# Attention scores in another PSUM pool, a second order for the last tiles' memory branch, and the sample recurrence's buffers swapped so that a weight load moves up

## The chip, the cores and the metric

The kernel runs on one core of a Trainium2 chip. The metric is the device time of one execution, in microseconds (us). Five engines run side by side: TensorE (PE, matmuls; PEld is its weight load), VectorE (DVE), ScalarE (ACT), GpSimd (POOL) and SyncE (SP, which here issues DMAs). Each works through its own instructions in order and waits on semaphores for the others.

## The reference, cut to what matters

One layer of a hybrid decoder for a prompt of 1,024 tokens and for 8 sequences of one new token each ("samples"). One projection of the normed input feeds three groups: NSA attention (8 query heads, 2 key/value heads; compressed blocks, selected blocks and a window of 512, mixed by gates), an RWKV-7 recurrence (4 heads) and attention into 256 memory tokens (4 heads). The groups are multiplied by SiLU gates, concatenated and projected out. The parts that the change touches:

```python
def masked_softmax(s, mask):                  # compressed, selected and window scores
    s = jnp.where(mask, s, -jnp.inf)
    m = jnp.max(s, axis=-1, keepdims=True)
    p = jnp.exp(s - m)
    return p / jnp.maximum(jnp.sum(p, axis=-1, keepdims=True), 1e-30)

def compress(rows2, pe, w1, b1, w2, b2):      # w1 is "w1a" in the kernel
    lo = einsum('ecpgd,epdh->ecgh', ch + pe[:, None, :CMP_STRIDE, None, :], w1[:, :CMP_STRIDE])
    hi = einsum('ecpgd,epdh->ecgh', ch + pe[:, None, CMP_STRIDE:, None, :], w1[:, CMP_STRIDE:])
    hid = silu(lo[:, :-1] + hi[:, 1:] + b1)
    ...
def step(s, inp):                             # RWKV-7, one token
    sa = einsum('bhvk,bhk->bhv', s, -kk_t)
    s = s * w_t + sa * b_t + v_t * k_t
    return s, einsum('bhvk,bhk->bhv', s, r_t)
# y is then normed per head, scaled, and a bonus r*k*r_k*v is added
```

## The kernel before, in words

The program has three phases. Phase 1 (to about 511 us) projects the prompt and runs its recurrence. Phase 2 (511 to 807 us) is the prompt's attention. Phase 3 (807 to the end) is the output projection, with the NSA attention of the 8 samples woven in.

**Phase 2.** The prompt has 8 tiles of 128 tokens, worked from tile i = 7 down to 0. Each tile has four units (2 key/value heads g, 2 head pairs hp), so there are 32 units n = 0 to 31. For a unit, `attn_scores` multiplies queries and keys into PSUM (p_s, in pieces of up to 512 keys; a split in high and low parts makes three matmuls of one product), VectorE masks them and takes the running maximum (`mask`, L1389, tile nm), ScalarE takes exp (L1399), VectorE the reciprocal of the sum (`scale`, L1403, tile fac), and POOL multiplies by it and by the gate (L1406). TensorE then transposes the probabilities (p_pT; `pt_copy` L1351 copies them to SBUF on ScalarE, L1360, or VectorE, L1362, as `self.turn` says) and multiplies by the values (p_o, L1447). Per tile there is also `attn_cmp` (compressed scores p_sc; VectorE's maximum L1324 and subtraction L1327 into pcq), `attn_rwkv` (p_yT) and `attn_mem` (memory scores p_sm; maximum nm_m L1484, exp into pmem L1486, POOL's scaling L1489, transposition p_pTm, copies ptm L1497, product p_om, addition to cat L1512).

PSUM has eight banks in phase 2: pool pS has two buffers of two banks for p_s, pool pT three of one bank for every transposition and, through the name pM, for p_sc, p_sm, p_om and others, and pO has one for p_o. A tile's buffer is reused only when all readers of its former tenant are done.

The order of the work is made in `phase2` (L1561). The units run in a loop; four generators are stepped between them at given rates: `query_tasks` (queries, compressed scores of the next tile), `tile_tasks` (recurrence output and memory branch of a tile), and `sample_tasks` with `sample_rest` (the samples' memory and window attention and their recurrence). Each yields the time that its step should have before the next is taken. `until(j, name)` steps generator j until it has reported `name`. The class `InOrder` keeps TensorE's instructions in the order in which they were written; the other engines are ordered by a scheduler's priorities.

**The samples.** `sample_rwkv` (L2142) is the recurrence of the 8 samples. It uses three SBUF arenas of 128 x 2048 (tags k0 to k2): a0 holds the state and a product, a1 (arena 1) the product t2, the inputs vk and the output column yv, a2 (arena 2) the rows vr and y. Its output goes through DRAM (sy_d) into another layout y, is normed (VectorE, L2280 and on) and transposed (p_sy). `nsa_ahead` (L1952), run behind it, loads what the samples' NSA attention needs first: the page table, the weights w1a into arena 2 (four DMAs, L1020), and the pages of sample 0, which a page table addresses: x (compressed rows) in arena 0 and kv in arena 1 (`pages`, L1937, L1950). SP issues these DMAs in its program order, and an issue that must wait for its target's readers holds up those behind it.

**Phase 3.** `sample_nsa` (L1966) loads the output weights as wraw (eight of 256 KB, L2299; cast and split into woh and wol at L2300 and L2301), v_new, then sample 1's pages and so on, all through SP. TensorE computes p_new, the compression of sample 0 (p_hid: pages times w1a), then output tiles of the prompt (p_out) with the compression of further samples between them.

## Time and profile before

| | us |
|---|---|
| median of 3 runs (lowest, highest) | 959.92 (959.6, 960.62) |
| profiled execution, its own time | 957.99 |
| span of that execution in the trace | 956.1 |

The mean granted clock of TensorE over the span is 0.990. The profile comes from the one execution in the third row. Busy times are per engine; a row of the timeline gives start, duration, engine, line, operation, written tile and read tiles, how many instructions it joins, and in brackets how long the engine stood idle before it and what released it. TensorE's instructions are recorded at L88 or L85 (the helper), so its rows are read by the tiles' names. The granted clock (1.00 is full) is the last but two of a table's columns; a DMA share of 1.00 means that all 16 DMA engines were busy.

### The profile page before, as it was taken

The page shows a single profiled execution, that of the slowest core. Times are in us where ns is not written, and L with a number is a line of the kernel's source. Part 1 is how long each engine was busy: PE and PEld are TensorE (multiplying, and loading weights), DVE is VectorE, ACT ScalarE, POOL GpSimd, SP SyncE. Part 2 cuts the span into 40 slices and gives each one's busy share as a digit, 9 for nine tenths or more (in the row PEclk, how much of TensorE's full clock was granted, in tenths as well). Part 3 has the DMA queues.
Part 4 walks back from the last instruction along what each step waited for, and adds up shares of the span by engine and source line. Part 5 has one row for each costly group of instructions (what it writes and reads, how often), then busy time and mean ns, then how long its engine had stood idle before and what let it go on. Part 6 is the DMA issues. An engine that isn't in the chain of part 4 may idle for free.

```text
span 956.1 us, 25353 instructions
## 1 busy us (share of the span) xinstructions
PE 907.5 (95%) x10095; PEld 754.5 (79%) x10095; DVE 650.5 (68%) x2146; ACT 431.8 (45%) x973; POOL 179.0 (19%) x262
## 2 busy tenths in 40 slices
PE   7999999999999999999997989999989988999998
PEld 7998888868898887778875767777877776787976
DVE  6668579847593799563447877677776895448564
ACT  7664324232442243222444666557567765324311
POOL 2000000000000000000001444444354765112111
PEclk9999999999999999999999999999999999999999
DMA  8521304321331127136327433240120043986561
GB/s 273 133 68 34 102 14 120 91 57 44 103 89 49 35 67 172 49 99 170 105 89 193 171 97 116 90 140 3 49 84 7 11 134 105 320 270 209 189 237 46
DMA packets 134989, 105.96 MB, mean 111 GB/s; under 512 B 34673, under 2 KB 121272, under 8 KB 134744
## 3 DMA queue, kind: packets, MB, share of 16 engines
q1 hardware_dynamic: 129880, 92.64, 32.7%
q0 software_dynamic: 3200, 10.49, 3.1%
q8 instruction: 79, 1.29, 0.6%
q10 hardware_dynamic: 1792, 1.23, 0.5%
q14 instruction: 38, 0.31, 0.1%
HBM read 85.74 MB, written 22.78 MB: 113 GB/s over the span
## 4 chain that ended last, share of the span: by engine, by line
PE 72%; DVE 16%; ACT 5%; DMA 3%; issue 3%; SPq 0%; POOL 0%; DVEq 0%; ACTq 0%; POOLq 0%
PE p_pr L88 19%; PE p_out L88 9%; PE p_pr L309 7%; PE p_o L88 5%; PE p_pT L88 5%; PE p_s L88 5%; PE p_hid L88 3%; DVE p L1389 3%; ACT p L1399 2%; PE p_iy L88 2%; PE p_z L88 1%; PE p_it L88 1%; PE p_mo L1137 1%; DVE wlo L286 1%; DMA w1a<-in_cmp_w_dram 1%
## 5 line engine op out<-in xcount | busy, mean ns | idle before, releaser
L88 PE MATMUL p_pr<-h,whi 128*128 128x512 f32 (+2 forms) x976 | 238.7, 337 | 0.0
L88 PEld LDWEIGHTS p_pr<-h,whi 128*128 128x128 f32 x976 | 157.7, 189 | 16.7 <-issue 2.8
L88 PE MATMUL p_pr<-h,wlo 128*128 128x512 f32 (+2 forms) x488 | 157.5, 326 | 0.6 <-DVE wlo L286 0.6
L1406 POOL TENSOR_SCALAR p<-p,fac,gates 128x640 f32<-128x640 f32 (+7 forms) x128 | 106.4, 843 | 126.8 <-DVE fac L1403 69.9
L1399 ACT ACTIVATE p<-p,nm 128x640 f32<-128x640 f32 (+7 forms) x128 | 92.7, 727 | 20.1 <-DVE nm L1389 18.2
L88 PEld LDWEIGHTS p_pr<-h,wlo 128*128 128x128 f32 x488 | 91.6, 189 | 9.1 <-DVE wlo L286 0.8
L88 PE MATMUL p_pT<-ident,p 128*128 128x128 f32 x528 | 72.4, 283 | 7.0 <-ACT pt L1360 2.5
L1389 DVE CUSTOM_DVE_ANT_0 p<-p_s,bmask 128x512 f32<-128x512 f32 (+3 forms) x128 | 64.4, 534 | 15.5 <-PE p_s L88 11.9
L1058 POOL MEMSET w2d<- 128x128 f32 x1 | 0.2, 205 | 393.0 <-PE p_yy L88 393.0
L88 PEld LDWEIGHTS p_pT<-ident,p 128*128 128x128 f32 x528 | 58.0, 143 | 19.0 <-issue 7.6
L309 PE MATMUL p_pr<-h,whi 128*128 128x264 f32 (+2 forms) x320 | 69.7, 311 | 0.0
L88 PE MATMUL p_o<-pt,vs 128*64 128x128 f32 x1056 | 68.8, 279 | 0.6 <-DVE cat L1464 0.6
L1360 ACT ACTIVATE pt<-p_pT 128x512 f32<-128x512 f32 (+1 forms) x82 | 46.9, 583 | 45.8 <-PE p_pT L88 45.5
L88 PEld LDWEIGHTS p_o<-pt,vs 128*64 128x64 f32 x1056 | 57.8, 138 | 9.1 <-issue 6.0
L286 DVE TENSOR_TENSOR wlo<-wraw,whi 128x1024 fp32r<-128x1024 f32 x33 | 40.4, 1223 | 31.7 <-ACT whi L285 31.7
L285 ACT ACTIVATE whi<-wraw 128x1024 fp32r<-128x1024 f32 x34 | 36.0, 1058 | 48.4 <-PE p_pr L88 35.7
L309 PEld LDWEIGHTS p_pr<-h,whi 128*128 128x128 f32 x320 | 51.4, 189 | 2.4 <-issue 0.2
L88 PE MATMUL p_out<-woh,chi 128*128 128x512 f32 x128 | 51.7, 404 | 0.0
L1362 DVE COPY pt<-p_pT 128x512 f32<-128x512 f32 (+1 forms) x62 | 41.1, 669 | 15.2 <-PE p_pT L88 15.0
L88 PE MATMUL p_out<-woh,clo 128*128 128x512 f32 x128 | 50.2, 392 | 0.4 <-DVE clo L2327 0.4
L88 PE MATMUL p_out<-wol,chi 128*128 128x512 f32 x128 | 50.1, 391 | 0.0
L309 PE MATMUL p_pr<-h,wlo 128*128 128x264 f32 (+2 forms) x160 | 49.3, 308 | 0.0
(552 smaller groups left out, 1880.0 us busy)
## 6 DMA issues: line engine op xcount, KB each, us to landing
wraw<-in_w_in_dram SPq DMA_DIRECT2D x34, 512.0 KB
pg<-in_c_pool_dram SPq DMA_DIRECT2D x32, 256.0 KB
pg<-in_c_pool_dram SPq DMA_DIRECT2D x48, 128.0 KB
x<-in_x_prompt_dram SPq DMA_DIRECT2D x8, 512.0 KB
z_d<-zt SPq DMA_DIRECT2D x16, 256.0 KB
cat<-z_d SPq DMA_DIRECT2D x8, 512.0 KB
xres<-in_x_prompt_dram POOLq DMA_DIRECT2D x16, 256.0 KB, 3.4
out_dram<-xres POOLq DMA_DIRECT2D x16, 256.0 KB, 3.4
```

Of the source, the lines that this page charges most:

```text
L88: self.last = getattr(self.engine, op)(*a, **k)
L285: nc.scalar.activation(hi[:, :, :n], raw[:, :, :n], AF.Copy)
L286: (low or nc.vector).tensor_tensor(lo[:, :, :n], raw[:, :, :n], hi[:, :, :n].bitcast(F32), op=OP.subtract)
L309: self.last_mm = self.pe.matmul(ps[:m, :b - a], w[:, k, :m], h[k][:, a:b], start=(k == 0 and i == 0), stop=(k == 7 and i == 2))
L1058: nc.gpsimd.memset(w2d[:], 0.0)
L1137: PE.matmul(po[t][:], a, w[:, j], start=(k + j == 0 and i == 0), stop=(k + j == 7 and i == 2))
L1360: self.last_copy = nc.scalar.activation(pt[:, :n], ps[:, :n], AF.Copy)
L1362: nc.vector.tensor_copy(pt[:, :n], ps[:, :n])
L1389: V.tensor_tensor_reduce(Ps[h, b][:, c0 - start:c1 - start], ps[:, h, :w], m, -1.0, nm[:, h, b, 0:1] if n else 3.0e38, op0=OP.add, op1=OP. ...
L1399: A.activation(x, x, AF.Exp, scale=-1.0, bias=nm[:, h, b, n:n + 1], accum_out=sm[:, h, b:b + 1])
L1406: nc.gpsimd.tensor_scalar(x, x, f[:, h, b:b + 1], gate[:, hd + h, 1 + b:2 + b], op0=OP.mult, op1=OP.mult)
```

## The change

- `attn_cmp` and `attn_mem` put their scores into one buffer of pool pS (half of two banks, and two banks) in place of two buffers of pool pT.
- `scale` issues its reciprocal only behind the last mask issued so far.
- `pt_copy` gives three of four copies to ScalarE in unit 0 too, where it was every second.
- In `phase2`, at unit 25, the queries of tile 0 and the memory branch of tile 1 are finished ahead of the unit's other work, with all that lies before them in their generators.
- In `sample_rwkv`, arenas 1 and 2 change places: t2, vk and yv lie in arena 2, the rows and y in arena 1. Six yields between its steps are gone.
- `nsa_ahead` is split: page table, w1a and sample 0's x pages are issued as soon as the recurrence's output is on its way through DRAM; the kv pages (arena 1) follow behind the recurrence.
- `START` gives the sample generator 0.5 in place of 0.7 before unit 0, and one yield in `attn_cmp` is 8.0 in place of 7.0. TensorE's order up to unit 25 is the same in both kernels.

```diff
@@ -37,7 +37,7 @@
 RATE = {i: (0.8, 0.8, 1, 1) if i > 3 else (1.5, 1.5, 1.8, 0) for i in range(8)}
 WAIT = (15.0, 5.0, 5.0, 0.0, 0.0, 0.0, 3.0, 0.0)
 WARM = (16, 15)
-START = (0.34, 0.0, 0.7, 0.0)
+START = (0.34, 0.0, 0.5, 0.0)
 PACE = 0.85
 EM = math.exp(-0.5)
 
@@ -1309,9 +1309,10 @@
         gate = self.gates[:, i, :].rearrange("p (h b) -> p h b", b=3)
         x = 56 - 8 * i
         half = [slice(h * 64, h * 64 + 64) for h in range(2)]
-        p2 = [self.pM.tile([128, 2, 2, 64], F32, name="p_sc", tag="m") for _ in range(2)]
+        two = self.pS.tile([128, 2, 512], F32, name="p_sc", tag="s")
+        p2 = [two[:, h, 0:256].rearrange("p (a b c) -> p a b c", a=2, b=2) for h in range(2)]
         for ps, o in zip(p2, half):
-            PE.matmul(ps[:].rearrange("p a b c -> p (a b) c"), self.cmask[o, 120:248],
+            PE.matmul(ps.rearrange("p a b c -> p (a b) c"), self.cmask[o, 120:248],
                       bc(self.cmask[o, None, x:x + 64], [64, 4, 64]), start=True, stop=False)
         for hp in range(2):
             for g in range(2):
@@ -1321,10 +1322,10 @@
         by = lambda x: x.rearrange("p (a h b) c -> p a h b c", a=2, h=2)
         st = self.small.tile([128, 8, 1], F32, name="c_m")
         for h, ps in enumerate(p2):
-            V.tensor_reduce(by(st[:])[:, :, h, :, 0], ps[:], axis=AX.X, op=OP.max)
+            V.tensor_reduce(by(st[:])[:, :, h, :, 0], ps, axis=AX.X, op=OP.max)
         V.tensor_scalar(st[:], st[:], -1.0e20, None, op0=OP.max)
         for h, ps in enumerate(p2):
-            V.tensor_tensor(by(pcq[:])[:, :, h], ps[:], bc(by(st[:])[:, :, h], [128, 2, 2, 64]), op=OP.subtract)
+            V.tensor_tensor(by(pcq[:])[:, :, h], ps, bc(by(st[:])[:, :, h], [128, 2, 2, 64]), op=OP.subtract)
         yield
         A.activation(pcq[:], pcq[:], AF.Exp)
         sm = self.small.tile([128, 8], F32, name="c_s")
@@ -1335,7 +1336,7 @@
         V.reciprocal(rc[:], rc[:])
         V.tensor_tensor(gh, gh, gate[:, :, 0].rearrange("p (g h) -> p g h", g=2), op=OP.mult)
         (G if i < 7 else V).tensor_tensor(pcq[:], pcq[:], bc(rc[:, :, None], [128, 8, 64]), op=OP.mult)
-        yield 7.0 if i < 7 else 4.0
+        yield 8.0 if i < 7 else 4.0
         self.pcT[i] = self.pt_copy(lambda j: pcq[:, 2 * j:2 * j + 2, :].rearrange("p a b -> p (a b)"), "c")
         yield
 
@@ -1356,7 +1357,7 @@
             self.te.transpose(ps[:, j, :], src(j), self.ident[:])
         pt = self.wk.tile([128, 4, 128], F32, name="pt", tag="pt" + tag, bufs=2 if tag == "c" else PTB)
         self.turn += 1
-        if self.turn % (2 if self.unit < 16 else 4):
+        if self.turn % (2 if 0 < self.unit < 16 else 4):
             self.last_copy = nc.scalar.activation(pt[:, :n], ps[:, :n], AF.Copy)
         else:
             nc.vector.tensor_copy(pt[:, :n], ps[:, :n])
@@ -1386,7 +1387,7 @@
         def mask(ps, h, b, n, c0, c1):
             w, start = c1 - c0, w0 if b else 0
             m = self.bmask[:, 1152 - w:1152] if c1 == n1 else self.bmask[:, 0:w] if b else self.bmask[:, 128:128 + w]
-            V.tensor_tensor_reduce(Ps[h, b][:, c0 - start:c1 - start], ps[:, h, :w], m, -1.0, nm[:, h, b, 0:1] if n else 3.0e38,
+            self.last_mask = V.tensor_tensor_reduce(Ps[h, b][:, c0 - start:c1 - start], ps[:, h, :w], m, -1.0, nm[:, h, b, 0:1] if n else 3.0e38,
                                    op0=OP.add, op1=OP.min, accum_out=nm[:, h, b, n:n + 1])
 
         f = self.small.tile([128, 2, 2], F32, name="fac")
@@ -1400,7 +1401,8 @@
             self.scales.append(lambda: scale(b, w))
 
         def scale(b, w):
-            V.reciprocal(f[:, :, b], sm[:, :, b])
+            with self.tc.issue_after(self.last_mask.ins):
+                V.reciprocal(f[:, :, b], sm[:, :, b])
             for h in range(2):
                 x = Ps[h, b][:, :w]
                 nc.gpsimd.tensor_scalar(x, x, f[:, h, b:b + 1], gate[:, hd + h, 1 + b:2 + b], op0=OP.mult, op1=OP.mult)
@@ -1469,7 +1471,8 @@
         qh, ql = self.qs[i]
         V, A, G, PE = nc.vector, nc.scalar, nc.gpsimd, self.te
         pms, pts = [], []
-        banks = [self.pM.tile([128, 2, 256], F32, name="p_sm", tag="m") for _ in range(2)]
+        two = self.pS.tile([128, 2, 512], F32, name="p_sm", tag="s")
+        banks = [two[:, h].rearrange("p (c k) -> p c k", c=2) for h in range(2)]
         for c in range(2):
             for n, (q, k) in enumerate(((qh, self.mkh), (qh, self.mkl), (ql, self.mkh))):
                 for h, ps in enumerate(banks):
@@ -1481,7 +1484,7 @@
             sm = self.small.tile([128, 2], F32, name="sm_m")
             pm = self.we.tile([128, 2, 256], F32, name="pmem", tag="pmem", bufs=2)
             pms.append(pm)
-            V.tensor_reduce(nm[:], ps[:], axis=AX.X, op=OP.max, negate=True)
+            V.tensor_reduce(nm[:], ps, axis=AX.X, op=OP.max, negate=True)
             for c in range(2):
                 A.activation(pm[:, c, :], ps[:, c, :], AF.Exp, bias=nm[:, c:c + 1], accum_out=sm[:, c:c + 1])
             V.reciprocal(sm[:], sm[:])
@@ -1547,8 +1550,9 @@
         while self.jobs:
             yield 1.0
         self.done.add("win")
-        yield from self.sample_rwkv()
-        yield from self.nsa_ahead()
+        ahead = self.nsa_ahead()
+        yield from self.sample_rwkv(ahead)
+        yield from ahead
 
     def sample_rest(self):
 
@@ -1656,6 +1660,9 @@
                             self.load_z(6)
                         if i > 0 and i < 7:
                             self.load_z(i - 1)
+                    if n == 25:
+                        until(0, ("q", 0))
+                        until(1, ("mem", 0))
                     pieces = sum(4 if units[m][0] >= 4 else 2 for m in ahead(n))
                     nxt = chain(*(scores(m) for m in ahead(n)))
                 later = turn(*groups[j + 1]) if j + 1 < len(groups) else None
@@ -1957,10 +1964,13 @@
         cd = self.cd = self.cs2.tile([128, 320], F32, name="c_dc")
         nc.sync.dma_start(cd[:], I["c_dc"])
         w1 = self.arena(2, "w1a")
+        x = self.arena(0, "pg")[:]
         with self.tc.high_priority(offset=2 * FIRST):
             self.load_w1([w1[:, e * 1024:e * 1024 + 1024].rearrange("p (j s h) -> p j s h", j=8, s=2) for e in range(2)])
-        self.pg = [self.arena(k, "pg")[:] for k in range(2)]
-        self.pages(0, *self.pg)
+        self.pages(0, x=x)
+        yield
+        self.pg = x, self.arena(1, "pg")[:]
+        self.pages(0, kv=self.pg[1])
         yield
 
     def sample_nsa(self):
@@ -2139,7 +2149,7 @@
             r = 0 if o is lo else 1
             V.tensor_tensor(c, c, x.rearrange("p s (c r) -> p r c s", r=2)[:, r], op=OP.mult)
 
-    def sample_rwkv(self):
+    def sample_rwkv(self, ahead):
         tc, nc, I, O = self.tc, self.nc, self.I, self.O
         V, A, G, PE = nc.vector, nc.scalar, nc.gpsimd, self.te
         b0, b1, b2 = (self.slot(j, [128, 1024], F32, f"rw_b{j}") for j in range(3))
@@ -2212,7 +2222,7 @@
         yield from wait(9.0)
         while self.unit < 16:
             yield 1.0
-        a0, a1, a2 = (self.arena(j, f"rw_a{j}") for j in range(3))
+        a0, a1, a2 = (self.arena(j, f"rw_a{j}") for j in (0, 2, 1))
         S, t = (a0[:, n:n + 1024].rearrange("p (a b) -> p a b", b=64) for n in (0, 1024))
         nc.sync.dma_start(a0[:, 0:1024], I["state_rwkv_wkv"][0].rearrange("s h (b v) k -> (s h b) (v k)", b=4))
         t2 = a1[:, 0:1024].rearrange("p (a b) -> p a b", b=64)
@@ -2241,19 +2251,15 @@
         kb = lambda j: bc(vk[:, j:j + 1, :], [128, 16, 64])
         vb = lambda x: bc(x[:, :, None], [128, 16, 64])
         V.tensor_tensor(t, S, kb(0), op=OP.mult)
-        yield 1.0
         V.tensor_tensor(S, S, kb(4), op=OP.mult)
         yield 1.0
         V.tensor_reduce(sa, t, axis=AX.X, op=OP.add)
-        yield 1.0
         V.tensor_tensor(t2, vb(vv), kb(2), op=OP.mult)
         yield 1.0
         V.tensor_tensor(S, S, t2, op=OP.add)
-        yield 1.0
         V.tensor_tensor(t, vb(sa), kb(1), op=OP.mult)
         yield 1.0
         V.tensor_tensor(S, S, t, op=OP.add)
-        yield 1.0
         V.tensor_tensor(t, S, kb(3), op=OP.mult)
         yield 1.0
         nc.sync.dma_start(O["wkv_sample"][0].rearrange("s h (b v) k -> (s h b) (v k)", b=4), a0[:, 0:1024])
@@ -2262,6 +2268,7 @@
         yd = tc.dram_tile([128, 16], F32, name="sy_d")
         nc.sync.dma_start(yd[:], yv)
         nc.sync.dma_start(y.rearrange("p h d -> p (h d)"), yd[:].rearrange("(s q) e -> s (q e)", s=NS))
+        next(ahead)
         h4 = lambda x: x.rearrange("p (h d) -> p h d", d=64)
         b4 = lambda x: bc(x[:, :, None], [NS, 4, 64])
         bn = self.small.tile([128, 4], F32, name="sbn")[:NS]
```

## The prediction, before the change was run

> **What bounds the kernel now.** I read the page first, then a table of stages, then the waits of TensorE, and last the timeline where it stands still. From the page, the busy times and the chain that ended last:
>
> ```profile
> PE 907.5 (95%) x10095; PEld 754.5 (79%) x10095; DVE 650.5 (68%) x2146; ACT 431.8 (45%) x973; POOL 179.0 (19%) x262
> PE 72%; DVE 16%; ACT 5%; DMA 3%; issue 3%; SPq 0%; POOL 0%; DVEq 0%; ACTq 0%; POOLq 0%
> ```
>
> TensorE is the bound, and the change takes no matmul from it. What can be won is its idle time and the time at half clock, so the stages matter (stretch, its length, then busy time and count per engine, granted clock, DMA share, GB/s):
>
> ```profile
> 511.00:521.00 10.00, 4.88 (x50) 3.66 (x52) 8.36 (x26) 4.29 (x11) 2.37 (x2) 1.00 0.73 206
> 521.00:525.00 4.00, 4.00 (x22) 3.40 (x20) 4.00 (x14) 2.81 (x7) 1.73 (x2) 0.57 0.97 250
> 560.00:650.00 90.00, 84.94 (x991) 66.61 (x989) 64.97 (x226) 55.13 (x131) 40.48 (x49) 1.00 0.37 113
> 650.00:750.00 100.00, 95.07 (x1067) 75.27 (x1063) 73.67 (x262) 69.32 (x176) 50.81 (x65) 1.00 0.13 36
> 750.00:782.00 32.00, 28.30 (x329) 23.00 (x325) 30.68 (x100) 23.59 (x73) 24.12 (x29) 1.00 0.22 70
> 784.40:787.80 3.40, 3.40 (x29) 2.95 (x29) 3.40 (x18) 2.89 (x10) 0.46 (x2) 0.52 0.37 90
> 795.00:807.00 12.00, 10.95 (x143) 8.58 (x144) 6.25 (x31) 8.63 (x28) 7.28 (x15) 1.00 0.20 58
> 807.00:811.00 4.00, 0.42 (x17) 0.36 (x15) 3.09 (x5) 0.77 (x1) 1.06 (x2) 0.64 1.11 306
> 811.00:815.00 4.00, 3.52 (x16) 3.22 (x16) 0.14 (x1) 0.27 (x1) 0.00 (x0) 0.50 1.10 313
> 820.00:834.00 14.00, 13.42 (x60) 10.66 (x59) 6.25 (x8) 3.40 (x5) 3.76 (x7) 1.00 0.93 309
> ```
>
> The idle time stands in four places: the start of attention (5.1 us of ten), its middle (5.1 of 90, 4.9 of 100, 3.7 of 32), its tail, and the handover to the sample stage, where TensorE does 0.42 us of work in four. After idle it runs at half clock (0.57, 0.52, 0.50). What it waits for in the whole run, and one wait of VectorE:
>
> ```profile
> PE p_hid L88 <- DMA w1a<-in_cmp_w_dram: 4.9, 2, 3.6
> PE p_s L88 <- DVE nm L1389: 4.5, 2, 3.8
> PE p_pT L88 <- ACT pt L1360: 2.5, 2, 1.6
> PE p_pT L88 <- DVE pcq L1327: 2.5, 3, 0.9
> PE p_sc L88 <- DVE pt L1362: 1.6, 1, 1.6
> PE p_sc L88 <- ACT pmem L1486: 1.3, 1, 1.3
> PE p_om L88 <- DVE cat L1512: 1.2, 1, 1.2
> PE p_pT L88 <- POOL pmem L1489: 0.8, 1, 0.8
> DVE fac L1403 <- ACT p L1399: 13.0, 20, 2.3
> ```
>
> The six rows of p_pT, p_sc and p_om I read as waits for one of three PSUM banks, which the transposes share with the compressed and memory scores (of the one put down to POOL this is an assumption: p_sm held a bank there too). The change gives these scores the window scores' two larger buffers.
>
> **Term 1, the start.** The last wait for nm, and two places like it further on:
>
> ```profile
> 520.79 0.50 PE L88 MATMUL p_s<-kh,qh 64*128 64x512 f32 x2 [3.81 <-DVE nm L1389]
> ...
> 711.50 0.48 PE L88 MATMUL p_s<-kh,qh 64*128 64x512 f32 x2
> ...
> 754.45 0.42 PE L88 MATMUL p_s<-kh,qh 64*128 64x384 f32 x1
> ```
>
> Here VectorE is the bound (8.36 of 10 us). Moving the reciprocal behind the last mask takes a wait of about 1.3 us from it, and the copies of unit 0 that go from VectorE to ScalarE take some 0.67 us each, most of them later than 525. But p_sc now occupies one of the two p_s buffers: the third p_s behind it waits for half of the subtraction L1328, so the same 3.8 us stand one p_s earlier, less what VectorE saves. I take +0.5 us (gains are positive). The lower end is 0; the upper is +2.2, if the idle is cut so far that the 4 us at clock 0.57 stay at full speed (1.7 us).
>
> **Term 2, the middle.** Gone, or mostly: 2.5 (pcq), 1.3 (pmem behind p_sc), 0.8 (POOL pmem), and about 0.9 of the 2.5 for pt and 0.6 of p_om's 1.2, together 6.1 us. ScalarE and VectorE, busy at most 74 us in 100, have room for the reads. New: the p_s behind a p_sc. It needs the buffer of the p_s ahead of p_sc, whose second mask ends here:
>
> ```profile
> 712.98 0.69 DVE L1389 CUSTOM_DVE_ANT_0 p<-p_s,bmask 128x512 f32<-128x512 f32 x1
> ...
> 755.01 0.55 DVE L1389 CUSTOM_DVE_ANT_0 p<-p_s,bmask 128x384 f32<-128x384 f32 x1
> ...
> 786.60 0.27 DVE L1389 CUSTOM_DVE_ANT_0 p<-p_s,bmask 128x128 f32<-128x128 f32 x1
> ```
>
> That is at 713.67 and 755.56, while p_s started at 711.50 and 754.45: new waits of 2.2 and 1.1 us. At the other places I put 1.0 in all. 6.1 − 4.3 = +1.8. Ends: −1, if each of the eight p_sm makes its follower wait 0.4 us more; +4, if the stream shifts so that half of the new waits are covered by the p_o matmuls that come next.
>
> **Term 3, the tail.** TensorE's order is written by hand; before, from the compressed scores of tile 0 on:
>
> ```order
> 2853 L88 MATMUL p_sc<-cmask 128x256 x2
> 2854 L88 MATMUL p_sc<-ck,q 128x64 x8
> 2855 L88 MATMUL p_s<-kh_6273,qh 128x128 x2
> 2856 L88 MATMUL p_s<-kl_6274,qh 128x128 x2
> 2857 L88 MATMUL p_s<-kh_6273,ql 128x128 x2
> 2858 L88 MATMUL p_pTm<-ident,pmem 128x128 x4
> 2859 L88 MATMUL p_s<-kh_6273,qh 128x128 x2
> ```
>
> And in the changed kernel, TensorE again, from the same p_sc to the second p_s behind it:
>
> ```order
> 2852 L88 MATMUL p_sc<-cmask 128x256 x2
> 2853 L88 MATMUL p_sc<-ck,q 128x64 x8
> 2854 L88 MATMUL p_pTm<-ident,pmem 128x128 x8
> 2855 L88 MATMUL p_yT<-ident,y_rw 128x128 x2
> 2856 L88 MATMUL p_om<-ptm,mv 64x128 x8
> 2857 L88 MATMUL p_sm<-mkh,qh 128x256 x2
> ...
> 2863 L88 MATMUL p_pT<-ident,p 128x128 x8
> 2864 L88 MATMUL p_s<-kh_6273,qh 128x128 x2
> ...
> 2867 L88 MATMUL p_s<-kh_6273,qh 128x128 x2
> ```
>
> Tile 1's p_pTm, p_yT and p_om and tile 0's p_sm now come in one block ahead of the unit's window scores. From the timeline of before, the p_sc and what comes at the stage's end:
>
> ```profile
> 782.26 0.38 PE L88 MATMUL p_sc<-cmask 64*128 64x256 f32 x1 [1.60 <-DVE pt L1362]
> ...
> 806.94 0.25 PE L88 MATMUL p_new<-s_o,qb 128*32 128x1 f32 x11
> ...
> 810.77 3.75 PE L88 MATMUL p_hid<-pg,w1a 128*128 128x128 f32 x16 [3.58 <-DMA w1a<-in_cmp_w_dram]
> 815.80 2.02 PE L88 MATMUL p_hid<-pg,w1a 128*128 128x128 f32 x16 [1.28 <-DMA w1a<-in_cmp_w_dram]
> 817.58 0.48 PE L88 MATMUL p_out<-woh,chi 128*128 128x512 f32 x1
> ...
> 833.60 3.81 PE L88 MATMUL p_hid<-pg,w1a 128*128 128x128 f32 x32 [0.58 <-issue]
> ```
>
> Won: the 1.60 us before p_sc (its bank is now a p_s buffer, long free), the half clock behind it (3.4 us at 0.52, that is 1.6), and 1.0 of the 1.05 us idle in 795 to 807, since memory's last steps no longer stand at the end: 4.2. Lost: about 0.5 us before p_om, for the copies of p_pTm, and a stall at the second p_s. That p_s needs the buffer of the p_s right ahead of it, because p_sm holds the other; so it waits for masks that VectorE's order puts behind the additions of both p_om, sums, p_sm's maximum and a copy. Three of these are passes over 512 columns:
>
> ```profile
> L1362 DVE COPY pt<-p_pT 128x512 f32<-128x512 f32 (+1 forms) x62 | 41.1, 669 | 15.2 <-PE p_pT L88 15.0
> ...
> L1484 DVE TENSOR_REDUCE nm_m<-p_sm 128x2 f32<-128x512 f32 x16 | 10.5, 680 | 0.6 <-PE p_sm L88 0.6
> ```
>
> So three by 0.68, two masks of 0.27, and ten smaller ones that I estimate at the masks' 0.27: 5.3 us from the last p_om on, while TensorE has 1.3 (p_sm), 1.1 (p_pT) and 0.5 (p_s) us to do: a stall of 2.4. 4.2 − 0.5 − 2.4 = +1.3. Ends: −2.5 (stall 4.2 and another half-clock window), +4 (no stall).
>
> The Trainium skill (TensorE: Matmul & The Clock Gate, Part 1) says that the clock falls to half after an idle window of about 3.4 us; the row shows it behind a wait of 1.60. By that rule the half clock would not hang on this wait, the 1.6 us would stay, and the term would be −0.3; the trace speaks for the row.
>
> **Term 4, the handover.** SP's queue before (each DMA once; a page's address load left out), around the weights w1a:
>
> ```order
> 235 L1950 DMA pg<-in_c_pool_dram 128x256
> 236 L1302 DMA cat_11116<-z_d 128x8x128
> 237 L2299 DMA wraw<-in_w_out_dram 128x512
> 238 L1020 DMA w1a<-in_cmp_w_dram 128x8x64 x4
> 239 L2299 DMA wraw<-in_w_out_dram 128x512 x7
> 240 L1981 DMA v_new<-out_dram 32x2x128 x4
> 241 L1942 TENSOR_LOAD pt
> 242 L1946 ISA
> 243 L1946 DMA pg<-in_c_pool_dram 128x2x256
> ```
>
> SP's queue in the changed kernel, at w1a and then from the third key/value page on:
>
> ```order
> 200 L1957 DMA pg<-in_c_pool_dram 128x256
> 201 L1020 DMA w1a<-in_cmp_w_dram 128x8x64 x4
> 202 L2270 DMA rw_a1_10321<-sy_d 8x256
> ...
> 230 L1957 DMA pg<-in_c_pool_dram 128x256
> 231 L2306 DMA wraw<-in_w_out_dram 128x512 x8
> 232 L1991 DMA v_new<-out_dram 32x2x128 x4
> ...
> 247 L1957 DMA pg<-in_c_pool_dram 128x256
> 248 L1949 TENSOR_LOAD pt
> 249 L1953 ISA
> 250 L1953 DMA pg<-in_c_pool_dram 128x2x256
> ```
>
> w1a moves some 30 us up, since its arena now holds buffers that the recurrence drops early. What waits for the norm's last read (p_sy) instead is the eight key/value pages, and all eight wraw stand behind the first three. SP's DMA issues before (start, time until the last ends, count):
>
> ```profile
> 772.51 10.30 SPq L1950 DMA_DIRECT2D pg<-in_c_pool_dram  x15
> ...
> 804.17 3.80 SPq L1020 DMA_DIRECT2D w1a<-in_cmp_w_dram  x4
> 808.03 6.01 SPq L2299 DMA_DIRECT2D wraw<-in_w_out_dram  x7
> 815.74 2.29 SPq L1981 DMA_DIRECT2D v_new<-out_dram  x4
> 818.64 11.52 SPq L1946 DMA_DIRECT2D pg<-in_c_pool_dram  x11
> ```
>
> Count from p_new at E = 806.9. Before, p_out starts at 817.58 = E + 10.7. Without the two waits, and with 32 p_hid in 3.8 us as at 833.60, it starts at E + 4.1: 6.6 us won. But the next p_hid (16.0 us behind p_out, so wanted at E + 20.1) needs sample 1's pages. Their issue starts after p_sy (about E − 3): eight wraw at 0.86 (6.9), v_new 2.3, eight pages at 0.69 to 1.05 (5.5 to 8.4), so at E + 11.7 to E + 14.6, where it was E + 11.7: not sooner. Before, those eight pages were issued by 827.0 (E + 20.1), and were used at E + 26.7, with DMA 0.93 busy; I put their landing 4 us behind the last issue, at E + 24, and the same after. So TensorE waits 3.9 us there and keeps 6.6 − 3.9 = +2.7. Ends: −2.8 (used as late as before, and issued 2.8 later), +6.6. The y load, now behind w1a's 3.8 us of issue, stays hidden: its first reader on VectorE ran at 780 or later.
>
> **Sum.** 0.5 + 1.8 + 1.3 + 2.7 = 6.3 us off the profiled execution's 957.99 (span 956.1 and 1.9 around it): 951.7. That execution is 1.9 below the median of the runs, 959.92; off the median it is **953.6**.
>
> **Rivals.** (a) Late pages take the handover back: sample 1's pages come when they did, and the wait is long enough for 32 p_hid at half clock (1.9 us lost). 3.6 − 1.9 = 1.7 won: 958.2. For it: DMA share 0.93 and an unmoved issue time. Against: w1a's 1 MB leaves the busiest stretch. (b) Slower: the window scores run on one buffer wherever p_sc or p_sm holds the other. Price: the 3.3 us of rows 711 and 754, 0.6 us at eight p_sm (4.8), against 6.1 gained: −2.0; in the tail a stall of 4.2 with a new half-clock window: −2.5; start 0, handover +1.1. Together −3.4: 963.3. It decides from the point where the new waits, 6.7 us in the forecast (4.3 and 2.4), come to 13. For it: VectorE is busy 30.68 of 32 us before the tail, so masks come late there. Against: in most of the middle it has a quarter of its time free. (c) More: no half clock at the start (+1.7), no tail stall (+2.4), pages 1.5 us sooner: 11.9 won, 948.0. (d) The half clock at 784 does not come from the wait there and stays (by the Trainium skill's rule above): 4.7 won, 955.2. (e) The arena is not free when SP comes to w1a and the load waits for p_sy as before: without term 4, 3.6 won, 956.3; against it, the recurrence's result leaves by 771.
>
> **Chances.** Forecast 0.46, (a) 0.16, (b) 0.15, (c) 0.13, (d) 0.06, (e) 0.04. A measurement here tells 0.2% (1.9 us) from nothing; so "same" is 958.0 to 961.8, which takes half of (a): 0.08. Slower is (b): 0.15; faster the rest: 0.77. The range leaves out (b) and the far part of (c): 947.5 to 960.0.
>
> **What would show it.** Right: no wait for w1a and p_out some 4 us behind p_new; a wait of 2 to 5 us on a page at the second p_hid; p_pT no longer waiting for pcq; p_s waiting for nm in two or three new places, one in the tail. Wrong: new waits of p_s over 13 us, a p_hid at half clock behind late pages, or p_out waiting for wraw, now issued behind p_sy.

## The result, and the profile after

The changed kernel is slower: 970.61 us (median of 8 runs, 966.53 to 972.65) against 961.87 (8 runs of the kernel before, 959.6 to 964.35). The ratio is 1.0087, 95% interval 1.0065 to 1.011, so about 8.4 us. The profiled executions took 969.58 and 957.99 us; the latter lies at the lower end of the runs of the kernel before (956.89 to 967.29 over the 25 runs of one comparison), so a difference of the two traces overstates the loss by some 3 us. Its mean granted clock, 0.990, is high too: the 104 later runs of the kernel before have 0.984 in the mean, the eight of the changed kernel 0.980.

The page after, busy times and the chain that ended last:

```profile
PE 917.1 (95%) x10095; PEld 761.1 (79%) x10095; DVE 649.8 (67%) x2143; ACT 433.3 (45%) x976; POOL 176.6 (18%) x262
PE 72%; DVE 14%; ACT 4%; DMA 3%; issue 3%; SPq 3%; POOL 1%; POOLq 0%; DVEq 0%; ACTq 0%
```

TensorE does the same 10,095 matmuls and is busy 9.6 us longer: the same work at a lower clock. SP's queue is new in the chain with 3%. The stages after (columns as before):

```profile
511.00:521.00 10.00, 5.65 (x54) 3.78 (x52) 8.32 (x30) 4.63 (x9) 2.38 (x2) 1.00 0.85 248
521.00:525.00 4.00, 4.00 (x38) 3.20 (x36) 3.92 (x17) 3.69 (x7) 2.17 (x2) 1.00 1.14 334
...
650.00:750.00 100.00, 93.38 (x1001) 73.56 (x1001) 71.22 (x247) 65.69 (x165) 45.94 (x58) 0.97 0.12 35
750.00:782.00 32.00, 28.82 (x313) 23.29 (x312) 26.98 (x84) 19.70 (x60) 18.52 (x25) 0.89 0.11 34
...
820.00:834.00 14.00, 12.80 (x43) 9.41 (x44) 8.34 (x15) 6.67 (x12) 2.69 (x5) 0.76 0.84 264
834.00:860.00 26.00, 22.86 (x126) 20.13 (x125) 8.20 (x18) 5.88 (x11) 2.78 (x6) 0.93 0.94 306
```

The start has gained its full clock in this trace (1.00 where it was 0.57). The middle has lost it (0.97 and 0.89 where it was 1.00), and so has the handover (0.76 and 0.93, also 1.00 before). From 807 to 815 it is the other way round: 0.64 and 0.50 before, 1.00 now. The rows of before that the prediction does not show, one of the stages and one of TensorE's waits:

```profile
834.00:860.00 26.00, 26.00 (x175) 22.19 (x174) 10.20 (x29) 6.94 (x16) 2.70 (x5) 1.00 0.88 282
...
PE p_pT L88 <- POOL p L1406: 0.9, 2, 0.7
```

What TensorE waits for after:

```profile
PE p_s L88 <- DVE nm L1390: 6.6, 5, 2.1
PE p_pT L88 <- POOL p L1408: 4.7, 8, 1.6
PE p_out L88 <- ACT woh L2307: 3.4, 1, 3.4
PE p_hid L88 <- issue: 3.1, 1, 3.1
PE p_s L88 <- DVE pcq L1328: 3.0, 1, 3.0
...
PE p_pT L88 <- ACT pt L1361: 2.2, 1, 2.2
PE p_sm L88 <- DVE nm L1390: 1.9, 1, 1.9
PE p_s L88 <- ACT pmem L1489: 1.1, 1, 1.1
PE p_sc L88 <- DVE nm L1390: 1.0, 2, 0.8
```

The waits for w1a (4.9) and for pcq in front of p_pT (2.5) are gone, as the change meant. In their place stand waits of the scores for p_s buffers, transpositions that wait for POOL (4.7 us in 8 places, where it was 0.9 in 2), p_out for woh, and the second p_hid (put down to "issue"; the chain of waits shows a page's DMA there). And VectorE's wait for ScalarE in front of the reciprocal, which was 13.0 us, is now:

```profile
DVE fac L1405 <- ACT p L1400: 3.7, 6, 1.4
```

Lengths by marks on TensorE's timeline (first p_s of attention, first queries p_q of tile 6, p_q of tile 0, p_new, second and third p_hid, end), in us:

| from, to | before | after | difference |
|---|---|---|---|
| first p_s, first p_q | 24.5 | 22.5 | -2.0 |
| first p_q, p_q of tile 0 (the middle) | 238.4 | 249.1 | +10.7 |
| p_q of tile 0, p_new (the tail) | 32.4 | 31.7 | -0.7 |
| p_new, second p_hid | 26.7 | 29.1 | +2.4 |
| second p_hid, third | 9.1 | 10.7 | +1.6 |
| third p_hid, end | 113.4 | 114.3 | +0.9 |

In the middle TensorE's idle time rose by 2.1 us (14.0 to 16.1, from the gaps of the timeline). The rest is clock: behind five of its waits stand stretches at half clock, and the trace of before has none in the middle:

```profile
553.86:557.27 3.41, 3.41 (x26) 2.97 (x28) 2.87 (x10) 1.65 (x5) 0.00 (x0) 0.50 0.68 229
622.13:625.54 3.41, 3.41 (x23) 1.52 (x24) 2.34 (x9) 0.34 (x1) 2.36 (x4) 0.50 0.02 5
714.29:717.70 3.41, 3.41 (x30) 3.08 (x27) 2.25 (x7) 2.13 (x5) 0.00 (x0) 0.50 0.01 2
727.94:731.35 3.41, 3.41 (x18) 2.12 (x19) 2.11 (x6) 2.00 (x5) 0.00 (x0) 0.50 0.12 38
758.66:765.49 6.83, 6.83 (x48) 5.29 (x46) 5.57 (x17) 2.70 (x7) 1.30 (x2) 0.50 0.01 2
```

The waits ahead of them, from TensorE's timeline:

```profile
553.84 0.58 PE L88 MATMUL p_sm<-mkh,qh 64*128 64x256 f32 x2 [1.86 <-DVE nm L1390]
...
621.95 0.45 PE L88 MATMUL p_s<-kh,qh 64*128 64x256 f32 x2 [2.96 <-DVE pcq L1328]
...
713.11 0.51 PE L88 MATMUL p_s<-kh,qh 64*128 64x512 f32 x2 [2.04 <-DVE nm L1390]
726.38 0.66 PE L88 MATMUL p_pT<-ident,p 128*128 128x128 f32 x4 [2.22 <-ACT pt L1361]
...
757.57 0.77 PE L88 MATMUL p_pT<-ident,p 128*128 128x128 f32 x5 [1.60 <-POOL p L1408]
```

Three are waits for a p_s buffer (554, 622 and 713; only the last stands where one was forecast), one is a transposition that waits for POOL, one a transposition behind a copy on ScalarE.

Part of the +10.7 is luck of the trace of before. Seven kernels of the experiments below leave the scores' buffers and the reciprocal as they were (only_copies, only_early_w1a, only_tail_order, early_w1a_late_kv, early_w1a_kv_later and its two filled forms). By the same marks their middle takes 241.5 to 243.9 us, in the median 241.9: idle 12.2 to 13.3, and 4.7 to 7.9 lost to half clock (half of the busy time in it). So the change costs the middle some 7 us, about 3 of idle time and 5 of clock, and not 10.7.

### The profile page after: what moved, and what is told of

It reads as the page before. It is cut to its first block, busy times and chain, and to the rows that moved or that the text cites. A ratio compares the mean times of both kernels' runs of the same rounds, so it can differ in the third digit from the quotient of the medians.

```text
span 967.8 us, 25326 instructions
## 1 busy us (share of the span) xinstructions
PE 917.1 (95%) x10095; PEld 761.1 (79%) x10095; DVE 649.8 (67%) x2143; ACT 433.3 (45%) x976; POOL 176.6 (18%) x262
## 3 DMA queue, kind: packets, MB, share of 16 engines
q1 hardware_dynamic: 129880, 92.64, 32.4%
## 4 chain that ended last, share of the span: by engine, by line
PE 72%; DVE 14%; ACT 4%; DMA 3%; issue 3%; SPq 3%; POOL 1%; POOLq 0%; DVEq 0%; ACTq 0%
PE p_pr L88 21%; PE p_pr L309 7%; PE p_out L88 7%; PE p_pT L88 5%; PE p_o L88 5%; PE p_s L88 5%; DVE p L1390 2%; PE p_hid L88 2%; PE p_iy L88 2%; PE p_z L88 1%; POOL p L1408 1%; PE p_it L88 1%; PE p_tk L88 1%; DVE wlo L286 1%; ACT p L1400 1%
## 5 line engine op out<-in xcount | busy, mean ns | idle before, releaser
L1408 POOL TENSOR_SCALAR p<-p,fac,gates 128x640 f32<-128x640 f32 (+7 forms) x128 | 102.6, 812 | 144.5 <-DVE fac L1405 88.4
L1400 ACT ACTIVATE p<-p,nm 128x640 f32<-128x640 f32 (+7 forms) x128 | 92.7, 727 | 19.3 <-DVE nm L1390 19.3
L88 PE MATMUL p_s<-kh,qh 64*128 64x512 f32 (+3 forms) x191 | 41.1, 423 | 10.6 <-DVE nm L1390 6.6
```

Of the source, the lines that this page charges most:

```text
L88: self.last = getattr(self.engine, op)(*a, **k)
L1400: A.activation(x, x, AF.Exp, scale=-1.0, bias=nm[:, h, b, n:n + 1], accum_out=sm[:, h, b:b + 1])
L1408: nc.gpsimd.tensor_scalar(x, x, f[:, h, b:b + 1], gate[:, hd + h, 1 + b:2 + b], op0=OP.mult, op1=OP.mult)
```

## The experiments

Every kernel is compared with runs of the kernel before on the same chip; ratios are to it. Theory 1 was mine after the two traces: the scores in the p_s buffers make the new waits, and half clock behind these is the loss. Theory 2, its rival: the moved reciprocal makes POOL late. Theory 3: the handover gives its win back through SP's queue.

### One part of the change alone

**only_scores_in_ps.**

```diff
-        p2 = [self.pM.tile([128, 2, 2, 64], F32, name="p_sc", tag="m") for _ in range(2)]
+        two = self.pS.tile([128, 2, 512], F32, name="p_sc", tag="s")
...
-        banks = [self.pM.tile([128, 2, 256], F32, name="p_sm", tag="m") for _ in range(2)]
+        two = self.pS.tile([128, 2, 512], F32, name="p_sm", tag="s")
```

> The kernel before, with one part of the change alone: the compressed and the memory scores in the window scores' two PSUM buffers. Theory 1 (new waits of the window scores for these two buffers, and a window of 3.4 us at half clock, 1.7 us lost, behind most of them): 7 to 11 us slower, with p_s or p_sm waiting 1 to 3 us in four or more new places between 550 and 800 us and at least four half-clock windows there. Rival theory 2 (the moved reciprocal makes POOL's scaling late and the transpositions wait): this kernel doesn't have that part, so within 2 us of before.

Measured: 967.46 us, ratio 1.0042 (1.0028 to 1.0056): 4.0 us slower. TensorE's waits for p_s buffers:

```profile
PE p_s L88 <- DVE nm L1390: 10.8, 8, 3.2
...
PE p_s L88 <- DVE pcq L1328: 3.3, 2, 3.0
PE p_sm L88 <- DVE nm L1390: 1.9, 1, 1.9
```

The waits are there, 4.5 us before and 16 now, but the loss is half of what theory 1 gave.

**only_reciprocal_and_copies**, and its two edits apart, **only_reciprocal** and **only_copies**.

```diff
-            V.reciprocal(f[:, :, b], sm[:, :, b])
+            with self.tc.issue_after(self.last_mask.ins):
+                V.reciprocal(f[:, :, b], sm[:, :, b])
...
-        if self.turn % (2 if self.unit < 16 else 4):
+        if self.turn % (2 if 0 < self.unit < 16 else 4):
```

> The kernel before, with the reciprocal issued behind the last mask, and three of four copies of unit 0 on ScalarE, alone. Theory 1: nothing is lost, 0 to 3 us faster, since VectorE no longer waits some 13 us for ScalarE. Rival theory 2 (late scaling on POOL): 4 to 8 us slower, with p_pT waiting 3 us or more for POOL in all.

> The kernel before with the reciprocal behind the last mask alone; unit 0's copies as before. Theory 2 (POOL's scaling comes late, the transpositions wait for it and half clock follows): nearly all of the 1.3% that both edits cost together, 8 to 13 us slower than before, with p_pT waiting 5 us or more for POOL. Rival theory 5 (the copies given to ScalarE in unit 0 delay the exps there): under 5 us slower.

> The kernel before with three of four copies of unit 0 on ScalarE, alone. Theory 2: within 2 us of before. Rival theory 5: 5 us slower or more, with half clock between 520 and 535 us.

Measured: together 976.64 us, 1.013 (1.0109 to 1.0151); the reciprocal alone 976.21, 1.0134 (1.0108 to 1.016), that is 12.9 us; the copies alone 962.28, 0.9992 (0.9973 to 1.0011). One line costs more alone than the whole change. The waits of the kernel with the reciprocal alone:

```profile
PE p_pT L88 <- POOL p L1407: 10.4, 14, 2.3
...
POOL p L1407 <- DVE fac L1404: 93.2, 32, 19.3
```

Theory 2 is right for this part: transpositions wait 10.4 us for POOL, in 14 places, and POOL waits 93.2 us for the reciprocals, where it was 69.9 (one of these waits alone is 19.3, at the start of attention; the longest before is 5.5). One such place, on VectorE, POOL and TensorE in turn:

```profile
796.33 0.15 DVE L1404 RECIPROCAL fac<-sm 128x2 f32<-128x2 f32 x1
```

```profile
796.68 2.19 POOL L1407 TENSOR_SCALAR p<-p,fac,gates 128x256 f32<-128x256 f32 x4 [1.74 <-DVE rq_t L138]
```

```profile
797.29 0.33 PE L88 MATMUL p_pT<-ident,p 128*128 128x128 f32 x1 [2.29 <-POOL p L1407]
```

ScalarE's exps nearest ahead of this reciprocal that had ended were over before 790.5 (its next ones run from 795.40, and their sum goes into the second reciprocal, at 796.53). So a finished sum lay some six microseconds behind four masks and the small operations of the samples' norm, POOL stood idle (1.74 us before its scaling, put down to the reciprocal's neighbour on VectorE), and TensorE behind POOL.

**only_early_w1a.**

```diff
-        a0, a1, a2 = (self.arena(j, f"rw_a{j}") for j in range(3))
+        a0, a1, a2 = (self.arena(j, f"rw_a{j}") for j in (0, 2, 1))
...
+        next(ahead)
```

> The kernel before, with the sample recurrence's arenas swapped and the early loads split off, alone. Theory 3 (the handover gives back more than it wins, since key/value pages and all eight wraw now stand behind the norm on SP): 2 to 5 us slower; no wait for w1a, but p_out waits about 3 us for woh and the second p_hid about 3 us for pages, with half clock behind both. Were the loss in the window scores' buffers alone, this kernel would be 2 to 6 us faster than before.

The edit also takes four yields out of the recurrence, as the change does (the diff has four, not six). Measured: 963.55 us, 1.0002 (0.9988 to 1.0016). No loss and no win. p_out waits little for woh here; from p_new to the second p_hid it takes 24.7 us against 26.7, 2.0 us less, where term 4 had 2.7; the tail gives it back (28.7 us from tile 0's p_sc to p_new against 26.6).

**only_tail_order.**

```diff
+                    if n == 25:
+                        until(0, ("q", 0))
+                        until(1, ("mem", 0))
```

> The kernel before, with tile 1's memory branch and tile 0's memory scores brought ahead of unit 25's other work, alone. Theory 1: the order in itself costs little, within 2 us of before, and no wait of p_s for the mask just ahead of it, since both p_s buffers are free for p_s. Rival (the block itself starves TensorE, whoever holds the buffers): 2 to 4 us slower, with a wait of about 2 us and a half-clock window between 785 and 800 us.

Measured: 965.55 us, 1.0031 (1.0015 to 1.0048), 3.0 us slower: between the two expectations. From p_new to the second p_hid it takes 28.7 us where it was 26.7, since p_sy now stands late in the order and w1a, not moved in this kernel, waits for it.

### The change without one part

**all_but_scores_in_ps, all_but_reciprocal, all_but_early_w1a, all_but_tail_order**, each the changed kernel with one edit taken back (the second also takes back the copies of unit 0, the third the yields of the recurrence):

```diff
-        two = self.pS.tile([128, 2, 512], F32, name="p_sm", tag="s")
...
-            with self.tc.issue_after(self.last_mask.ins):
...
-        a0, a1, a2 = (self.arena(j, f"rw_a{j}") for j in (0, 2, 1))
...
-                    if n == 25:
```

> The changed kernel with the compressed and memory scores back in the pool of the transpositions. Theory 1: 7 to 11 us faster than the changed kernel, so within 3 us of before; the half-clock windows between 550 and 800 us go from six to two at most. Rival theory 2 (late scaling on POOL): it stays 5 us or more above before.

> The changed kernel without the moved reciprocal and without the moved copies of unit 0. Theory 1: as slow as the changed kernel or slower, 8 to 12 us above before. Rival theory 2: 4 to 8 us faster than the changed kernel, with p_pT waiting for POOL 1 us in all where it was 4.7.

> The changed kernel with the sample recurrence's arenas and the early loads as before. Theory 3 (the handover loses): 2 to 5 us faster than the changed kernel; p_hid waits for w1a again, p_out no longer for woh, nor the second p_hid for pages. Against theory 3: no faster or slower than the changed kernel.

> The changed kernel without the new order at unit 25. Theory 1: the wait of 1.5 us for the buffer that p_sm holds and the half-clock window at 796 go, and others of the same kind come; within 2 us of the changed kernel. Rival (the block starves TensorE): 2 to 4 us faster.

| kernel | median us | ratio to before | interval |
|---|---|---|---|
| changed | 970.61 | 1.0087 | 1.0065 to 1.011 |
| all_but_scores_in_ps | 973.99 | 1.0115 | 1.0085 to 1.0146 |
| all_but_reciprocal | 970.14 | 1.0079 | 1.0048 to 1.011 |
| all_but_early_w1a | 976.94 | 1.014 | 1.0109 to 1.0171 |
| all_but_tail_order | 970.32 | 1.0073 | 1.0045 to 1.0101 |

Theory 1 falls here: with the scores taken back nothing is won. Theory 2 doesn't hold in its simple form either: without the reciprocal nothing is won. Theory 3 falls as well in this comparison: without the early load the kernel is some 0.5% slower than the changed one, with intervals that just touch. No single part carries the loss.

**changed_without_either** takes both back, the scores' buffers and the reciprocal:

```diff
-        two = self.pS.tile([128, 2, 512], F32, name="p_sc", tag="s")
-        two = self.pS.tile([128, 2, 512], F32, name="p_sm", tag="s")
...
-            with self.tc.issue_after(self.last_mask.ins):
```

> The changed kernel with both the scores' buffers and the reciprocal as before; the rest of the change stays. If the two parts share one loss (either alone is enough to make TensorE wait, both together are little worse): 5 to 8 us faster than the changed kernel, 0 to 0.35% above before. If the rest (tail order, early loads) carries the loss: as slow as the changed kernel, 0.7 to 0.9% above before.

Measured: 965.52 us, 1.0026 (1.001 to 1.0041). The pair holds 0.61 of the 0.87%, 5.9 us; alone its parts cost 4.0 and 12.9. So they share one loss. The length of the middle, by the marks above, says where it lies:

| kernel | middle, us |
|---|---|
| changed | 249.1 |
| all_but_reciprocal | 245.9 |
| all_but_scores_in_ps | 246.5 |
| changed_without_either | 241.9 |
| only_scores_in_ps | 244.1 |
| only_reciprocal | 251.1 |

Without either part it is as long as in the seven kernels that have neither. How the two parts keep each other's loss small is only read from the waits, and no run tests it: transpositions wait for POOL 10.4 us with the reciprocal alone and 4.7 with both, and p_s waits for nm 10.8 us with the scores alone and 6.6 with both. VectorE, no longer held up in front of a reciprocal, ends its masks sooner and frees p_s buffers; TensorE, held up at these buffers, gives POOL time.

### The handover

**early_w1a_late_kv, changed_late_kv and early_w1a_kv_later** move sample 0's key/value pages on SP from behind the norm to behind the pages of sample 2 (the last one: sample 3). The first and the last stand on the kernel before and take the arenas and the early load of the change, with the recurrence's yields as before; the second stands on the changed kernel.

```diff
         self.pg = x, self.arena(1, "pg")[:]
-        self.pages(0, kv=self.pg[1])
...
                                 load(s)
+                            if s == 2:
+                                self.pages(0, kv=self.pg[1])
                             squeeze(s, hid)
```

> The kernel before with the arenas swapped and the early loads, the recurrence's yields as before, and sample 0's key/value pages moved behind the pages of sample 2 in place of right behind the norm. Theory 3 (what the early w1a wins is given back because eight pages and then wraw stand between the norm and sample 1's pages): the second p_hid no longer waits 3 us for pages, and the time from p_new to it falls from 24.7 to 20 to 22 us (26.7 before): 4 to 7 us faster than before. Rival (the transfers are the limit there, in whatever order): the second p_hid waits as long, within 2 us of before.

> The changed kernel with sample 0's key/value pages moved behind the pages of sample 2. Theory 3: the waits of p_out for woh (3.4 us) and of the second p_hid for pages (3.1 us), and the half clock behind them, go or shrink: 4 to 8 us faster than the changed kernel, within 5 us of before. Rival: 0 to 2 us faster, since the transfers are the limit.

> The kernel before with the arenas swapped and the early loads, and sample 0's key/value pages behind the pages of sample 3 in place of sample 2. With them behind sample 2, the fourth p_hid waited 2.4 us for pages and ran at half clock after it (4.2 us). If that was the queue: this wait goes, and the time from p_new to the fifth p_hid falls from 84.2 to 80 us (87.7 before); 3 to 8 us faster than before. If the transfers are the limit: the wait moves to the sample scores p_ss behind it, within 2 us of before.

Measured: early_w1a_late_kv 962.8 us, 1.0002 (0.9979 to 1.0024); changed_late_kv 967.78, 1.004 (1.0022 to 1.0059), which takes half of the change's loss away; early_w1a_kv_later 956.74, 0.9925 (0.9901 to 0.9948), faster than both kernels. The order in SP's queue was the limit, not the sum of the transfers: from 812 to 836 us the DMA engines are no less busy in early_w1a_kv_later (shares of 0.88 to 1.05 in steps of 6 us) than in the changed kernel (0.65 to 1.01). SP after the change (start, time until the last ends):

```profile
811.40 2.01 SPq L1957 DMA_DIRECT2D pg<-in_c_pool_dram  x3
813.51 4.98 SPq L2306 DMA_DIRECT2D wraw<-in_w_out_dram  x8
820.58 3.77 SPq L1991 DMA_DIRECT2D v_new<-out_dram  x4
824.87 3.83 SPq L1957 DMA_DIRECT2D pg<-in_c_pool_dram  x5
829.33 27.42 SPq L1953 DMA_DIRECT2D pg<-in_c_pool_dram  x24
```

And SP in early_w1a_kv_later:

```profile
802.20 3.66 SPq L2305 DMA_DIRECT2D wraw<-in_w_out_dram  x8
812.97 1.75 SPq L1984 DMA_DIRECT2D v_new<-out_dram  x4
815.30 28.62 SPq L1947 DMA_DIRECT2D pg<-in_c_pool_dram  x24
844.44 7.69 SPq L1951 DMA_DIRECT2D pg<-in_c_pool_dram  x9
```

Nothing waits for the norm ahead of wraw, and sample 1's pages (the first of the 24) start 2.5 us behind p_new, where it was 15.7. TensorE there:

```profile
813.23 3.81 PE L88 MATMUL p_hid<-pg,w1a 128*128 128x128 f32 x32
816.79 0.48 PE L88 MATMUL p_out<-woh,chi 128*128 128x512 f32 x1
...
831.87 3.73 PE L88 MATMUL p_hid<-pg,w1a 128*128 128x128 f32 x32
840.93 3.73 PE L88 MATMUL p_hid<-pg,w1a 128*128 128x128 f32 x32
```

No wait in front of any of them: p_out starts 4.0 us behind p_new (812.84), and from p_new to the fifth p_hid it takes 80.1 us, before 87.7. With the pages behind sample 2, the fourth p_hid waited 2.4 us and ran at half clock, and that time was 84.2.

### Dummy matmuls in the waits

**reciprocal_with_filled_waits (and _2)** puts matmuls of the identity, whose result the next transposition overwrites, in front of 16 transpositions of only_reciprocal; **early_w1a_kv_later_fill (and _2)** puts them into the wait at the start of attention. The _2 kernels have half as many.

```diff
+            for _ in range(FILL.get((self.turn, j), 0)):
+                self.te._do("matmul", ps[:, j, :], self.ident[:], self.ident[:], start=True, stop=True)
             self.te.transpose(ps[:, j, :], src(j), self.ident[:])
```

> The kernel before with the reciprocal behind the last mask alone, and 111 dummy matmuls on TensorE (about 0.11 us each, 12 us in all, into PSUM that the next transposition overwrites) just ahead of the 16 transpositions that waited in that kernel's trace, a little less in each place than the wait. Nothing else changes, and VectorE, POOL and ScalarE have the same work. If half clock follows from a lack of busy time in a window of 3.4 us: the half-clock windows behind these waits go, and the kernel is 4 to 8 us faster than with the reciprocal alone (0.5 to 0.9% above before, where that one was 1.34%). If half clock has another cause: as slow as with the reciprocal alone, or slower by what the dummies overrun, 1.2 to 1.6% above before.

> As reciprocal_with_filled_waits, with 55 dummy matmuls in place of 109; by that run's trace one takes 0.23 us, so 12.7 us in all, in 16 waits that came to 13.8 us. If half clock follows from lost busy time: no half-clock window behind the filled waits, and 3 to 7 us faster than with the reciprocal alone (0.6 to 1.0% above before, where that one was 1.34%). If not: as slow as that one, or slower.

> As early_w1a_kv_later, with 28 dummy matmuls (3 us) in TensorE's wait of 3.8 us for the masks at the start of attention. If half clock follows from lost busy time: no half-clock window between 518 and 526 us in any run's profile, and 0.5 to 2 us faster than early_w1a_kv_later (VectorE is busy all through that window and may keep part of it). Otherwise no faster.

> As early_w1a_kv_later_fill, with 14 dummy matmuls (3.3 us) in place of 28, in the wait of 3.8 us at the start. If half clock follows from lost busy time: no half-clock window there, and the first stretch of attention, 24.6 us in early_w1a_kv_later, takes 22.5 to 23.5 us; the whole 0 to 2 us faster than early_w1a_kv_later, the fastest so far. If not: 24.5 us or more in that stretch, no faster.

Measured: with too many dummies 983.21 us, 1.0189 (1.0162 to 1.0216), and 957.11, 0.994 (0.9922 to 0.9958); with half as many 976.3, 1.0132 (1.0112 to 1.0152), and 956.98, 0.9939 (0.9923 to 0.9955). The dummies' size in the first pair was my error (0.23 us each):

```profile
519.59 6.52 PE L88 MATMUL p_w<-ident 128*128 128x128 f32 x56
```

That is 28 dummies, two passes each, in a wait of 3.8. In both kernels with filled transpositions no half clock is left behind a filled wait: the stretches at half clock in attention stand behind waits that were not filled (from 538.8, 562.7 and 634.4 in the first, from 540.3, 560.8 and 632.5 in the second). But the time did not follow. In the _2 kernel, from the first p_s to the end, 55 dummies added 12.9 us of work, idle time fell by 5.7 and half of the time at half clock by 6.8, and the total stayed (462.7 us, and 463.1 with the reciprocal alone). Of the dummies 7.2 us thus came on top of what was idle, about as much as the clock gave back, and the run can't tell whether fuller clock alone would have saved time. In the start it was 26.3 us in place of 24.6, with half clock at 528.2, behind a wait of 2.18 that was not filled. So that lost busy time brings half clock is shown; that half clock by itself sets the time in these places is not.

## Why the prediction was wrong

**The step that failed is the sum of term 2, the middle**, put at +1.8 us, where the change costs some 7. Where it said what the change costs there, it had the scores' buffers alone; the reciprocal stood only in term 1, as a wait taken from VectorE. It asked who waits for VectorE's masks, and not who waits for the reciprocal: POOL, and behind POOL the transpositions. The row that should have warned was on the page of before, POOL's scaling, idle 69.9 us for fac:

```profile
L1406 POOL TENSOR_SCALAR p<-p,fac,gates 128x640 f32<-128x640 f32 (+7 forms) x128 | 106.4, 843 | 126.8 <-DVE fac L1403 69.9
```

Alone the moved reciprocal costs 12.9 us, more than every term of the sum. But it is only part of the step: without it the changed kernel is still 0.79% above before. The other part is the price of the scores' buffers, too low in the same sum. With either part taken back alone the kernel stays as slow, and only without both does the middle come back to 241.9 us.

**The new waits for p_s buffers were right in kind, and half right in place.** Forecast were 2.2 us at 711, which came as 2.04 at 713.11, and 1.1 at 754, which did not come. Instead 1.86 came at 553.84, where p_sm itself waits, 2.96 at 621.95, and 1.13 at 751.66, behind p_sm, where the sum had 1.0 for all other places. Together that is 8.0 us in the middle for 4.3, and 9.5 with the tail: below the 13 at which the prediction let its sum turn. And no half clock was counted behind any of them, though the prediction priced just that at the start and in the tail. The waits that were to go did go (for pcq, and the p_sc near 624).

**Term 1** (+0.5, ends 0 to +2.2): the start is 2.0 us shorter, its half clock gone in this trace. One of 3.4 us stands at 554 instead. changed_late_kv and all_but_tail_order, with the same edits to the start, take 24.3 and 24.0 us there, with 6.8 us at half clock, so most of the 2.0 is luck.

**Term 3** (+1.3): 0.7 us shorter. The stall for the p_s buffer came as 1.51 us at 794.81, with half clock behind it.

**Term 4** (+2.7, ends -2.8 to +6.6): -2.4 to the second p_hid and -1.6 for the half clock behind it (from 844.0). p_out did not start at E + 4.1 but at E + 7.6: woh was late, since wraw stood behind p_sy, the risk named last. Sample 1's pages started at E + 15.7, later than the E + 11.7 to E + 14.6 forecast, and p_hid took them at E + 29.1. Rival (a) is the one that happened there, and worse than priced. Two of the prediction's three signs of being wrong came here; the third, waits of p_s over 13 us, did not.

**Rival (b)** had the sign. Its mechanism is one part of the cause: the scores' buffers cost 4.0 us alone, but the reciprocal alone 12.9, and the two share 5.9 us of the 8.4. The other 2.5 us (changed_without_either) belong to the rest, in shares that single kernels don't separate: alone the tail's order costs 3.0, the early load and the copies 0. START and the yield of 8.0 in `attn_cmp` were not run apart.

**The clock rule weighed in term 3**: the Trainium skill (TensorE: Matmul & The Clock Gate, Part 1) has half clock follow an idle window of about 3.4 us. In these traces waits of 1.5 to 3 us are enough, so the measurement decides against reading that window as unbroken idle time.

## What to carry to other kernels

When an instruction is moved later on its engine, ask first who consumes its result, and follow that chain to the engine that sets the time; the wait that the move saves on its own engine may be worth nothing. Two buffers shared by more tenants move a wait rather than remove it. When a load is moved ahead of a barrier, look at what takes its place behind the barrier, and put there what is needed last. A single trace of the kernel before can be a lucky one: compare a stretch with the same stretch in other kernels that leave it alone.

## What the runs showed of the hardware

Half clock comes in steps of 3.41 us on a fixed grid: in each of the 20 traces, the starts of all stretches at half clock lie a whole number of such steps apart, to within 0.01 us. Cutting each trace from 40 to 950 us by its own grid, full-speed steps in which TensorE was busy under 45% were followed by half clock in 54 of 54 cases, 45 to 50% in 33 of 42, 50 to 65% in 26 of 78, above that in 11 of 4,988. Where the grid lies against the program differs from trace to trace. A wait of 2 us therefore costs half clock in one trace and not in another: the two waits before p_sc at 623 to 625 us, 0.99 and 1.33, brought none in the trace of before and 6.8 us of it in that of only_copies, which has the same waits there. This would explain why runs of one kernel spread over 10 us: of the 104 runs of the kernel before, the fastest (956.89 us) has a mean granted clock of 0.993, the slowest (968.27) 0.979. That the grid's place is the reason wasn't tested.
